# Half-array products for the query's low part in a hybrid attention layer

## The chip, the cores and the metric

The kernel runs on one NeuronCore of a Trainium2 chip. The metric is the device time of one execution in microseconds, the median of several executions. Five engines work side by side, each through a queue of its own: TensorE (PE, with its weight loads shown apart as PEld), VectorE (DVE), ScalarE (ACT), GpSimd (POOL) and SyncE (SP), which issues the transfers here.

## What is computed

One decoder layer over 2048 tokens of 1024 channels: a normalised and modulated `h`, one input projection of 4096 columns, two kinds of causal attention, an output projection and a gated residual. Eight heads of 64 use stick-breaking attention, four heads use differential attention, whose two maps have queries and keys of 64 each.

```python
def _stick_breaking(q, k, v):
        z = jnp.einsum('bhqd,bhkd->bhqk', qb, kf) * inv
        mask = spos[None, :] < tpos[:, None]
        log_1m = jnp.where(mask, jax.nn.log_sigmoid(-z), 0.0)
        rem = lax.cumsum(log_1m, axis=3, reverse=True) - log_1m
        a = jnp.where(mask, jnp.exp(jax.nn.log_sigmoid(z) + rem), 0.0)
        return jnp.einsum('bhqk,bhkd->bhqd', a, vf)

def _diff_attention(q1, q2, k1, k2, v, lam, slopes):
        s1 = jnp.einsum('bhqd,bhkd->bhqk', qb1, k1f) * inv + bias
        s2 = jnp.einsum('bhqd,bhkd->bhqk', qb2, k2f) * inv + bias
        p1 = jax.nn.softmax(jnp.where(mask, s1, -jnp.inf), axis=-1)
        p2 = jax.nn.softmax(jnp.where(mask, s2, -jnp.inf), axis=-1)
        return jnp.einsum('bhqk,bhkd->bhqd', p1 - lam * p2, vf)
```

## The kernel before

All large products take float32r operands. To keep precision each value is split into a high part (rounded to float32r) and a low part (the remainder), and products of parts are added in PSUM. `split_store` makes the two parts of projected queries and keys and writes them to DRAM (`qst`, `kst`); `ev_qk` calls it for the stick-breaking heads, `ev_dqk` for the differential ones. The tokens are worked on in two halves of 1024, and each half in chunks (`ch`) of 512.

`load_k` brings one chunk of 512 keys as a tile `kc` of 128 rows: 64 rows of the high part, below them 64 rows of the low part. `load_q` brings a pair of query tiles twice, on rows 0 to 63 and on rows 64 to 127, with the high part in slot 0 and the low part in slot 1. So in `scores` (L482) one product with slot 0 as weights gives q-high times (k-high + k-low) over all 128 rows, and a second one with slot 1 adds q-low times (k-high + k-low). In the stick-breaking heads the chunk on the diagonal gets a third product (L485), 128 wide, of an identity with a mask. Each product has its own weight load.

A row is one tile of 128 queries `i` against its `(i + 1) * 128` keys, in up to four chunks of up to 512 keys (`segs`; a last piece of 128 is computed 256 wide). The scores of a chunk lie in `ps_z`, a PSUM tile with three buffers (`NZ`). In the stick-breaking heads (`SBHead.front`) the chunks run from the last to the first; ScalarE makes two sigmoids of a chunk (L613, L614), VectorE scans it (L617), which is the last reader of `ps_z`, and GpSimd multiplies (L621). In the differential heads (`DFHead.front`) they run from the first to the last, and VectorE adds the bias and takes the maximum (L699), the only reader.

When two rows (a pair of query tiles) are done, `back_steps` turns the weights by 128x128 transposes into `ps_t` (L518), splits them into `aH` and `aL` (L524 on ScalarE, L525 on VectorE), and multiplies by the values into `av` (`vmm`: L598 and L599, or L671 to L673), 256 columns for two query tiles at a time. For the last key tile of a pair the first 128 columns belong to queries ahead of the keys; there `aH` and `aL` are set to zero by two memsets on GpSimd (L522, L523).

The order is set in two steps. A planner at the end of `build` lists the attention steps (`A`), each with a cost, and lets steps of the projections (`P`) in between by due times; `aper` sums an estimate of PE's time over the attention steps that issue a product, and projection steps are tied behind the product issued about `WINDOW` (17 us) earlier. Then the framework's scheduler orders each engine's queue by a forecast of its own. On the chip each queue runs in that order.

Of the kernel before, what the change touches and what calls it, by code (L numbers as in the profile page):

```python
# [7 lines left out]
F32 = mybir.dt.float32  # L8
# [37 lines left out]
def build(ctx: ExitStack, tc, xT, cT, normg, w_adaT, b_ada, w_in, qg, kg, lam4, subg, w_out,  # L46
          identd, distd, outT):
    nc = tc.nc
# [7 lines left out]
    zps = ctx.enter_context(tc.tile_pool(name="zps", bufs=NZ, space=PSUM))  # L56
# [12 lines left out]
    identr = ctile([128, 128], "ident", F32R)  # L69
# [12 lines left out]
    maskr = ctile([128, 128], "maskr", F32R)  # L82
# [270 lines left out]
    def ev_qk(dst, base):  # L353
        def f(ps, c, half, ch):
            p = (c - base) // 128
            t = dst[p][half]
            split_store(ps, [t[:, i, :, ch * 512:ch * 512 + 512] for i in range(2)])
        return f

    def ev_gate(ps, c, half, ch):  # L360
# [59 lines left out]
    def ev_dqk(isq):  # L420
        state = {}

        def f(ps, c, half, b2):
            qn = stage("qn")
            nc.scalar.copy(qn, ps)
            sq = stage("sq")
            nc.scalar.activation(sq, ps, AF.Square)
            if b2 % 2 == 0:
                state["ss"] = col.tile([128, 16], F32, name="qss", tag="qss", bufs=2)
                state["t"] = []  # L430
            ss = state["ss"]
            nc.vector.reduce_sum(out=ss[:, (b2 % 2) * 8:(b2 % 2) * 8 + 8],
                                 in_=sq.rearrange("p (u d) -> p u d", d=64), axis=AX.X)
            state["t"].append(qn)
            if b2 % 2 == 0:
                return
            v = col.tile([128, 16], F32, name="qv", tag="qv", bufs=1)
            nc.vector.tensor_scalar(out=v, in0=ss, scalar1=1.0 / 64, scalar2=EPS,
                                    op0=ALU.mult, op1=ALU.add)
            y = rsqrt(v, 16)  # L440
            tl = state["t"]
            for i in range(2):
                q3 = tl[i].rearrange("p (u d) -> p u d", d=64)
                nc.gpsimd.tensor_tensor(out=q3, in0=q3,
                                        in1=y[:, i * 8:i * 8 + 8].unsqueeze(2).broadcast_to([128, 8, 64]),
                                        op=ALU.mult)

            def finish(ch=b2 // 2):
                for s in range(2):
                    tp = pps.tile([128, 512], F32, name="ps_q", tag="pj")  # L450
                    for j in range(4):
                        o = (j % 2) * 256 + s * 128
                        nc.tensor.transpose(tp[:, j * 128:(j + 1) * 128], tl[j // 2][:, o:o + 128],
                                            ident)
                    hd = (c - (C_DFQ if isq else C_DFK)) // 128 + s
                    t = (qst if isq else kst)[4 + hd][half]
                    split_store(tp, [t[:, i, :, ch * 512:ch * 512 + 512] for i in range(2)],
                                qgain[:, hd:hd + 1] if isq else kgt[:, 0:1])
            pending.append([QK_DELAY, finish])
        return f  # L460
# [17 lines left out]
    def scores(q, kch, i, k0, w, diag=None):  # L478
# [7 lines left out]
                                          stop=True)  # L486
        return ps

    def segs(n, ext):
        return [(o, min(512, n - o), min(512, ext - o, max(256, n - o))) for o in range(0, n, 512)]  # L490

    def chunks(i):
        L = (i + 1) * 128
# [7 lines left out]
    def back_steps(pair, A, get_av, acol, vmm):  # L501
        i1 = 2 * pair + 1
        ng = i1 // 2 + 1

        def up(st, g):
            last = g == ng - 1
            tp = tps.tile([128, 512], F32, name="ps_t", tag="tr")
            aH = apool.tile([128, 512], F32R, name="aH", tag="aH", bufs=NA)
            aL = apool.tile([128, 512], F32R, name="aL", tag="aL", bufs=NA)
            blk = []  # L510
            for sl in range(2):
                sb = 2 * g + sl
                pos = (1 - sl) if last else sl
                blk.append((sb, pos * 256))
                for t in range(2):
                    if last and sl == 1 and t == 0:
                        continue
                    nc.tensor.transpose(tp[:, pos * 256 + t * 128:pos * 256 + t * 128 + 128],  # L518
                                        A[t][0][:, sb * 128:sb * 128 + 128], ident)
            f0 = 128 if last else 0  # L520
            if last:
                nc.gpsimd.memset(aH[:, 0:128].bitcast(F32), 0.0)  # L522
                nc.gpsimd.memset(aL[:, 0:128].bitcast(F32), 0.0)  # L523
            nc.scalar.copy(aH[:, f0:], tp[:, f0:])  # L524
            nc.vector.tensor_tensor(out=aL[:, f0:], in0=tp[:, f0:], in1=aH[:, f0:].bitcast(F32),  # L525
                                    op=ALU.subtract)
            st["h"] = (blk, aH, aL)

        def down(st, gi):
            av = get_av()  # L530
            blk, aH, aL = st["h"]
            for bi, (sb, o) in enumerate(blk):
                vmm(av[:, acol:acol + 256], sb, aH[:, o:o + 256], aL[:, o:o + 256],
                    gi == 0 and bi == 0, gi == ng - 1 and bi == 1)

        res = []
        sts = [{} for _ in range(ng)]
        for gi in range(ng + PIPE):
            def step(gi=gi):
                if gi < ng:  # L540
                    up(sts[gi], ng - 1 - gi)
                if gi >= PIPE:
                    down(sts[gi - PIPE], gi - PIPE)
            res.append((0.62 if gi < ng else 0.0, step))
        return res
# [34 lines left out]
    class SBHead(Head):  # L580
# [15 lines left out]
        def vmm(self, o, sb, aH, aL, st, sp):  # L596
            v = self.vch[sb // 4][:, sb % 4]
            nc.tensor.matmul(o, lhsT=v, rhs=aH, start=st, stop=False)  # L598
            last_pe[0] = nc.tensor.matmul(o, lhsT=v, rhs=aL, start=False, stop=sp)  # L599

        def front(self, i, A):
            steps = []
            tiles = {}

            def step(c0, w, we, first):
                self.open()
                q = self.get_q(i // 2)
                if first:
                    tiles["u"], tiles["s"] = self.row("u", i), self.row("s", i)
                u, s = tiles["u"], tiles["s"]  # L610
                dg = i * 128 - c0
                ps = scores(q, self.kch, i, c0, we, dg if 0 <= dg < w else None)
                nc.scalar.activation(s[:, c0:c0 + w], ps[:, :w], AF.Sigmoid, scale=0.125)  # L613
                nc.scalar.activation(ps[:, :w], ps[:, :w], AF.Sigmoid, scale=-0.125)  # L614
                top = c0 + w == L
                ur = ps[:, :w][:, ::-1]
                nc.vector.tensor_tensor_scan(out=u[:, c0:c0 + w][:, ::-1], data0=ur, data1=dist[:, :w],  # L617
                                             initial=1.0 if top else u[:, c0 + w:c0 + w + 1],
                                             op0=ALU.mult, op1=ALU.bypass)
                m = w - 1 if top else w  # L620
                nc.gpsimd.tensor_tensor(out=s[:, c0:c0 + m], in0=s[:, c0:c0 + m],  # L621
                                        in1=u[:, c0 + 1:c0 + m + 1], op=ALU.mult)

            L = (i + 1) * 128
            ext = (i // 2 + 1) * 256
            for si, (c0, w, we) in enumerate(reversed(segs(L, ext))):
                steps.append((2 * w / 960, lambda c0=c0, w=w, we=we, f=si == 0: step(c0, w, we, f)))

            def mid():
                A[0] = tiles["s"]  # L630
            return steps, (0.2, mid)
# [20 lines left out]
    class DFHead(Head):  # L652
# [27 lines left out]
        def front(self, i, A):  # L680
# [3 lines left out]
            nk = len(cl)  # L684
            ns = (128 * i + 639) // 512
            st = {}
            e = [None, None]

            def step(m, ci, c0, o, w, we, first):
                self.open()  # L690
                q = self.get_q(i // 2)[m]
                if "mx" not in st:
                    st["mx"] = col.tile([128, 2, ns], F32, name="mx", tag="mx")
                if first:
                    e[m] = self.row(f"e{m}", i)
                ps = scores(q, self.kch[m], i, c0 + o, we)
                d0 = 1920 - 128 * i + c0 + o
                j = (c0 + o) // 512
                nc.vector.tensor_tensor_reduce(  # L699
                    out=e[m][:, c0 + o:c0 + o + w], in0=ps[:, :w], in1=dist[:, d0:d0 + w], scale=1.0,  # L700
                    scalar=-3e38, op0=ALU.add, op1=ALU.max, accum_out=st["mx"][:, m, j:j + 1])
# [513 lines left out]
```

## Time and profile before

| | us |
|---|---|
| median of 3 executions | 1756.36 (1751.09 to 1757.32) |
| the profiled execution | 1752.65 |
| its span, first to last instruction | 1750.9 |
| busy: PE, PE's weight loads | 1657.7, 1486.7 |
| busy: VectorE, ScalarE, GpSimd | 1258.4, 990.3, 890.0 |

The stages in order of time: a start of 137 us, stick-breaking heads of half 0 up to 475 us, differential heads of half 0 up to 718, stick-breaking heads of half 1 up to 1250, differential heads of half 1 up to 1642, and a tail. Projections run beside the attention throughout. Recorded ends of matmuls are modelled; starts are what to read.

### The profile page before, as it was taken

How to read it: one execution, taken by the hardware profiler on the slowest of the kernel's cores; microseconds unless marked ns; L12 is line 12 of the kernel's file. 1: busy time of each engine (PE TensorE's matmuls, PEld its weight loads, DVE VectorE, ACT ScalarE, POOL GpSimd, SP SyncE). 2: the span in 40 equal slices, each digit the busy share in tenths (PEclk: the TensorE clock that was granted, in tenths of full speed). 3: DMA queues.
4: the chain of work that ended last, by engine and by line, in shares of the span. 5: the costliest groups of instructions: out<-in, count | busy, mean ns of one | idle time of the engine just before them, and what ended most of it. 6: DMA issues, size and time to landing. Idle time of an engine off the chain costs nothing.

```text
span 1750.9 us, 31674 instructions
## 1 busy us (share of the span) xinstructions
PE 1657.7 (95%) x10740; PEld 1486.7 (85%) x10740; DVE 1258.4 (72%) x2558; ACT 990.3 (57%) x1997; POOL 890.0 (51%) x1454
## 2 busy tenths in 40 slices
PE   1889989999999999999999999999999999999999
PEld 1677879789999989878898888799998988888887
DVE  6735645776657786767787877878888888888741
ACT  2335555555645444656776777777765645555521
POOL 5425464556635663565655655667433353323553
PEclk7999999999999999999999999999999999999999
DMA  7757767653564876434433333234433566434264
GB/s 254 228 151 211 217 187 226 190 163 85 164 181 135 254 240 187 157 106 121 121 101 105 97 109 97 79 94 131 133 88 116 162 204 203 130 127 134 86 216 149
DMA packets 212689, 268.65 MB, mean 153 GB/s; under 512 B 21296, under 2 KB 136240, under 8 KB 212400
## 3 DMA queue, kind: packets, MB, share of 16 engines
q1 hardware_dynamic: 212528, 266.64, 50.5%
q8 instruction: 85, 1.39, 0.3%
q14 instruction: 76, 0.62, 0.1%
HBM read 186.86 MB, written 79.69 MB: 152 GB/s over the span
## 4 chain that ended last, share of the span: by engine, by line
PE 69%; DVE 6%; DMA 4%; POOL 3%; issue 3%; ACT 2%; SPq 0%; DVEq 0%; ACTq 0%; POOLq 0%
PE ps_z L482 11%; PE ps_t L518 8%; PE ps_n L318 6%; PE ps_n L320 6%; PE ps_n L319 6%; PE ps_p L318 4%; PE ps_p L320 4%; PE ps_p L319 4%; PE av L599 3%; PE av L598 3%; PE ps_o L319 3%; PE ps_o L318 3%; PE ps_o L320 3%; PE av L672 1%; DMA xt<-in_xT 1%
## 5 line engine op out<-in xcount | busy, mean ns | idle before, releaser
L621 POOL TENSOR_TENSOR s<-s,u 128x512 f32<-128x512 f32 (+4 forms) x320 | 307.2, 962 | 213.1 <-DVE u L617 190.0
L482 PE MATMUL ps_z<-kc,qc 128*128 128x512 f32 (+2 forms) x1280 | 360.3, 376 | 9.4 <-DVE u L617 6.9
L524 ACT CAST aH<-ps_t 128x512 fp32r<-128x512 f32 (+1 forms) x432 | 240.7, 567 | 169.3 <-PE ps_t L518 159.5
L525 DVE TENSOR_TENSOR aL<-ps_t,aH 128x512 fp32r<-128x512 f32 (+1 forms) x432 | 276.3, 650 | 76.3 <-ACT aH L524 74.3
L318 PE MATMUL ps_n<-wh,hH 128*128 128x256 f32 x960 | 274.4, 286 | 2.4 <-DVE sl L327 1.2
L306 POOL TENSOR_TENSOR wl<-raw,wh 128x512 fp32r<-128x512 f32 x168 | 225.8, 1352 | 93.2 <-ACT wh L302 85.4
L319 PE MATMUL ps_n<-wl,hH 128*128 128x256 f32 x960 | 271.6, 284 | 1.0 <-POOL wl L306 1.0
L320 PE MATMUL ps_n<-wh,hL 128*128 128x256 f32 x960 | 272.3, 284 | 0.0
L617 DVE TENSOR_TENSOR_SCAN u<-ps_z,u,dist 128x512 f32<-128x512 f32 x192 | 245.6, 1279 | 33.8 <-ACT ps_z L614 27.7
L482 PEld LDWEIGHTS ps_z<-kc,qc 128*128 128x128 f32 x1280 | 210.9, 189 | 36.5 <-DVE u L617 11.9
L713 ACT ACTIVATE e<-e,nm 128x1024 f32<-128x1024 f32 (+4 forms) x192 | 171.9, 898 | 116.4 <-DVE nm L711 109.0
L699 DVE CUSTOM_DVE_ANT_0 e<-ps_z,dist 128x512 f32<-128x512 f32 (+3 forms) x320 | 186.9, 603 | 52.0 <-PE ps_z L482 44.5
L613 ACT ACTIVATE s<-ps_z 128x512 f32<-128x512 f32 (+3 forms) x320 | 172.9, 540 | 75.6 <-PE ps_z L482 38.9
L318 PE MATMUL ps_p<-hH,wh 128*128 128x512 f32 x480 | 192.5, 405 | 12.0 <-issue 11.2
L319 PE MATMUL ps_p<-hL,wh 128*128 128x512 f32 x480 | 189.7, 395 | 3.7 <-DVE hL L251 2.3
L320 PE MATMUL ps_p<-hH,wl 128*128 128x512 f32 x480 | 189.2, 395 | 0.0
L318 PEld LDWEIGHTS ps_n<-wh,hH 128*128 128x128 f32 x960 | 183.0, 191 | 6.9 <-issue 1.6
L319 PEld LDWEIGHTS ps_n<-wl,hH 128*128 128x128 f32 x960 | 183.2, 191 | 4.5 <-POOL wl L306 1.2
L320 PEld LDWEIGHTS ps_n<-wh,hL 128*128 128x128 f32 x960 | 183.3, 191 | 1.7
L614 ACT ACTIVATE ps_z<-ps_z 128x512 f32<-128x512 f32 (+3 forms) x320 | 173.2, 541 | 0.0
L518 PE MATMUL ps_t<-ident,s 128*128 128x128 f32 x1088 | 167.6, 274 | 5.2 <-DVE aL L525 4.9
L598 PE MATMUL av<-aH,vc 128*128 128x256 f32 x576 | 162.5, 294 | 7.4 <-ACT aH L524 6.3
(171 smaller groups left out, 3500.3 us busy)
## 6 DMA issues: line engine op xcount, KB each, us to landing
qc<-qst SPq DMA_DIRECT2D x256, 128.0 KB, 3.2
raw<-in_w_in SPq DMA_DIRECT2D x124, 256.0 KB, 3.3
kc<-kst SPq DMA_DIRECT2D x96, 256.0 KB, 3.5
xt<-in_xT SPq DMA_DIRECT2D x48, 256.0 KB, 4.7
vc<-vst SPq DMA_DIRECT2D x48, 256.0 KB, 3.1
vc<-vdt SPq DMA_DIRECT2D x48, 256.0 KB, 3.6
raw<-in_w_out SPq DMA_DIRECT2D x48, 256.0 KB, 3.4
wada<-in_w_adaT SPq DMA_DIRECT2D x16, 512.0 KB, 5.8
```

The source lines that it names most:

```text
L306: nc.gpsimd.tensor_tensor(out=wl, in0=raw, in1=wh.bitcast(F32), op=ALU.subtract)
L318: nc.tensor.matmul(ps, lhsT=aH, rhs=bH, start=first, stop=False)
L319: nc.tensor.matmul(ps, lhsT=aH, rhs=bL, start=False, stop=False)
L320: nc.tensor.matmul(ps, lhsT=aL, rhs=bH, start=False, stop=last)
L482: last_pe[0] = nc.tensor.matmul(ps[:, :w], lhsT=q[:, pt, tl], rhs=kch[k0 // 512][:, :w], start=pt == 0, stop=pt == 1 and diag is None)
L518: nc.tensor.transpose(tp[:, pos * 256 + t * 128:pos * 256 + t * 128 + 128], A[t][0][:, sb * 128:sb * 128 + 128], ident)
L524: nc.scalar.copy(aH[:, f0:], tp[:, f0:])
L525: nc.vector.tensor_tensor(out=aL[:, f0:], in0=tp[:, f0:], in1=aH[:, f0:].bitcast(F32), op=ALU.subtract)
L598: nc.tensor.matmul(o, lhsT=v, rhs=aH, start=st, stop=False)
L617: nc.vector.tensor_tensor_scan(out=u[:, c0:c0 + w][:, ::-1], data0=ur, data1=dist[:, :w], initial=1.0 if top else u[:, c0 + w:c0 + w + 1], ...
L621: nc.gpsimd.tensor_tensor(out=s[:, c0:c0 + m], in0=s[:, c0:c0 + m], in1=u[:, c0 + 1:c0 + m + 1], op=ALU.mult)
L699: nc.vector.tensor_tensor_reduce(out=e[m][:, c0 + o:c0 + o + w], in0=ps[:, :w], in1=dist[:, d0:d0 + w], scale=1.0, scalar=-3e38, op0=ALU.a ...
```

## The change

Odd chunks of keys are stored, and so loaded, with the low part on rows 0 to 63 and the high part on rows 64 to 127; even chunks stay as they were. A new function `scores2` takes an even and an odd neighbouring chunk together: two products with q-high over all 128 rows, then two with q-low, each over only the 64 rows that hold its chunk's high keys (rows 0 to 63 for the even one, 64 to 127 for the odd one). The product of both low parts is thereby left out for paired chunks. Both `ps_z` tiles are made at the first step of the pair; the second step finds its scores ready and issues no product. A chunk without a partner goes through `scores` as before. Row ends of 128 are computed 128 wide, and so is the product into `av` for a pair's last key tile, whose memsets go except where a pair has one group only.

```diff
--- before.py
+++ after.py
@@ ev_qk
-            split_store(ps, [t[:, i, :, ch * 512:ch * 512 + 512] for i in range(2)])
+            sw = ch if dst is kst else 0
+            split_store(ps, [t[:, i ^ sw, :, ch * 512:ch * 512 + 512] for i in range(2)])
@@ ev_dqk
-                    split_store(tp, [t[:, i, :, ch * 512:ch * 512 + 512] for i in range(2)],
+                    sw = 0 if isq else ch
+                    split_store(tp, [t[:, i ^ sw, :, ch * 512:ch * 512 + 512] for i in range(2)],
@@
+    def scores2(q, kch, i, parts, diag):
+        tl = slice((i % 2) * 128, (i % 2) * 128 + 128)
+        pss = {}
+        for k0, w in parts:
+            pss[k0] = zps.tile([128, 512], F32, name="ps_z", tag="z")
+            last_pe[0] = nc.tensor.matmul(pss[k0][:, :w], lhsT=q[:, 0, tl], rhs=kch[k0 // 512][:, :w],
+                                          start=True, stop=False)
+        for k0, w in parts:
+            r = slice(64 * (k0 // 512 % 2), 64 * (k0 // 512 % 2) + 64)
+            dg = diag - k0 if 0 <= diag - k0 < w else None
+            last_pe[0] = nc.tensor.matmul(pss[k0][:, :w], lhsT=q[r, 1, tl], rhs=kch[k0 // 512][r, :w],
+                                          start=False, stop=dg is None)
+        for k0, w in parts:
+            if 0 <= diag - k0 < w:
+                last_pe[0] = nc.tensor.matmul(pss[k0][:, diag - k0:diag - k0 + 128], lhsT=identr,
+                                              rhs=maskr, start=False, stop=True)
+        return pss
+
     def segs(n, ext):
-        return [(o, min(512, n - o), min(512, ext - o, max(256, n - o))) for o in range(0, n, 512)]
+        return [(o, min(512, n - o), min(512, n - o)) for o in range(0, n, 512)]
@@ back_steps
-            if last:
+            if last and ng == 1:
                 nc.gpsimd.memset(aH[:, 0:128].bitcast(F32), 0.0)
                 nc.gpsimd.memset(aL[:, 0:128].bitcast(F32), 0.0)
@@
-                vmm(av[:, acol:acol + 256], sb, aH[:, o:o + 256], aL[:, o:o + 256],
+                n0 = 128 if ng > 1 and gi == 0 and bi == 1 else 0
+                vmm(av[:, acol + n0:acol + 256], sb, aH[:, o + n0:o + 256], aL[:, o + n0:o + 256],
                     gi == 0 and bi == 0, gi == ng - 1 and bi == 1)
@@ SBHead.front
-                ps = scores(q, self.kch, i, c0, we, dg if 0 <= dg < w else None)
+                if c0 in ready:
+                    ps = ready.pop(c0)
+                elif c0 // 512 % 2:
+                    ready.update(scores2(q, self.kch, i, [(c0, w), (c0 - 512, 512)], i * 128))
+                    ps = ready.pop(c0)
+                else:
+                    ps = scores(q, self.kch, i, c0, we, dg if 0 <= dg < w else None)
@@ DFHead.front
-                ps = scores(q, self.kch[m], i, c0 + o, we)
+                k0 = c0 + o
+                if k0 in ready:
+                    ps = ready.pop(k0)
+                elif k0 // 512 % 2 == 0 and k0 + 512 < (i + 1) * 128:
+                    ready.update(scores2(q, self.kch[m], i, [(k0, w), (k0 + 512, min(512, (i + 1) * 128 - k0 - 512))],
+                                         -1))
+                    ps = ready.pop(k0)
+                else:
+                    ps = scores(q, self.kch[m], i, k0, we)
```

## Rows read from the trace of the kernel before

**Rows 1.** The page: busy time by engine (share), then 40 equal slices in tenths.
```profile
PE 1657.7 (95%) x10740; PEld 1486.7 (85%) x10740; DVE 1258.4 (72%) x2558; ACT 990.3 (57%) x1997; POOL 890.0 (51%) x1454
...
PE   1889989999999999999999999999999999999999
...
PEclk7999999999999999999999999999999999999999
```

**Rows 2.** Stages: start:end, length, busy us (xcount) by engine, granted clock, DMA.
```profile
core 0: us, PE busy (x) PEld busy (x) DVE busy (x) ACT busy (x) POOL busy (x), PEclk, DMA share, GB/s
...
137.00:475.00 338.00, 325.82 (x2090) 292.92 (x2089) 206.38 (x308) 190.81 (x403) 192.22 (x294) 0.99 0.61 178
475.00:718.00 243.00, 238.58 (x1710) 221.67 (x1709) 173.64 (x553) 124.54 (x268) 121.44 (x294) 1.00 0.67 197
718.00:1250.00 532.00, 519.58 (x3484) 468.26 (x3483) 419.81 (x521) 385.10 (x773) 325.76 (x437) 1.00 0.37 109
1250.00:1642.00 392.00, 384.38 (x2510) 345.22 (x2509) 340.96 (x965) 219.76 (x437) 141.32 (x305) 1.00 0.45 140
```

**Rows 3.** Waits of PE: who waited for whom, us in total, times, longest.
```profile
PE ps_z L482 <- DVE u L617: 6.9, 13, 0.7
...
PE ps_z L482 <- DVE mx L699: 2.2, 4, 0.9
```

**Rows 4.** PE's groups by shape: busy us, mean ns of one, idle before, releasers.
```profile
L482 PE MATMUL ps_z<-kc,qc 128*128 128x512 f32 x896 | 282.6, 404 | 8.4 <-DVE u L617 6.3 <-DVE mx L699 1.9
...
L482 PE MATMUL ps_z<-kc,qc 128*128 128x256 f32 x256 | 53.8, 291 | 1.1 <-DVE u L617 0.7 <-DVE mx L699 0.4
L482 PE MATMUL ps_z<-kc,qc 128*128 128x384 f32 x128 | 34.0, 344 | 0.0
```

**Rows 5.** Timeline of PE near 1001 us: start, us, instruction.
```profile
1000.12 0.39 PE L319 MATMUL ps_p<-hL,wh 128*128 128x512 f32 x1
1000.35 0.40 PE L320 MATMUL ps_p<-hH,wl 128*128 128x512 f32 x1
...
1001.96 0.39 PE L318 MATMUL ps_p<-hH,wh 128*128 128x512 f32 x1
```

**Rows 6.** Timeline of PE and its loads near 357 us.
```profile
356.89 0.23 PE L485 MATMUL ps_z<-maskr,ident 128*128 128x128 f32 x1
...
356.96 0.33 PE L598 MATMUL av<-aH,vc 128*128 128x256 f32 x1
357.01 0.19 PEld L599 LDWEIGHTS av<-aL,vc 128*128 128x128 f32 x1
357.13 0.28 PE L599 MATMUL av<-aL,vc 128*128 128x256 f32 x1
357.13 0.19 PEld L598 LDWEIGHTS av<-aH,vc 128*128 128x128 f32 x1
357.25 0.28 PE L598 MATMUL av<-aH,vc 128*128 128x256 f32 x1
357.25 0.19 PEld L599 LDWEIGHTS av<-aL,vc 128*128 128x128 f32 x1
357.36 0.28 PE L599 MATMUL av<-aL,vc 128*128 128x256 f32 x1
```

**Rows 7.** The first memset of `aH`: durations ns, idle before it, who waited.
```profile
L522 POOL MEMSET aH<- x96: 194/205/221, 0.7 to 1653.6; 128x128 f32 x96
...
  PE av L598: 64.0, 26
...
  ACT aH L524: 0.5, 1
```

**Rows 8.** Timeline near 773 us, stick-breaking, half 1: where two chunks of a row begin.
```profile
771.85 1.08 PE L482 MATMUL ps_z<-kc,qc 128*128 128x512 f32 x4
...
772.35 2.67 DVE L617 TENSOR_TENSOR_SCAN u<-ps_z,u,dist 128x512 f32<-128x512 f32 x2 [1.04 <-ACT ps_z L614]
...
773.68 0.73 PE L482 MATMUL ps_z<-kc,qc 128*128 128x512 f32 x2 [0.69 <-DVE u L617]
```

More of the change, by code (lines that the diff above doesn't have):

```diff
@@ L603, in front @@
             tiles = {}
+            ready = {}
             def step(c0, w, we, first):
@@ L686, in front @@
             st = {}
+            ready = {}
             e = [None, None]
```

## The prediction

> **What bounds the kernel now.** I read the page's busy shares first, then the same by stage, then who made TensorE wait, then single products in the timeline. TensorE (PE) is busy for 95% of the span, and from the second of the 40 slices on it stands at 8 or 9 tenths, with a granted clock of 9 tenths or more [rows 1]. By stage (stick-breaking heads of half 0, differential heads of half 0, then both for half 1) PE is busy 325.82 of 338, 238.58 of 243, 519.58 of 532 and 384.38 of 392 us, at a clock of 0.99 to 1.00, which is the 2.4 GHz level. VectorE is next, at most 340.96 of 392 us [rows 2]. All attention products lie in these 1505 us, so there a microsecond of PE is a microsecond of span, as long as no wait takes its place. Waits of PE at the score products are small today: 6.9 us for the scan and 2.2 us for the differential heads' reduction [rows 3].
>
> A record's duration is no price, since a 512-wide product is recorded at 404 ns and the next one starts long before that [rows 4]. The price is the distance between starts. Eight products of 512 columns from 1000.12 to 1001.96 us give 1.84/8 = 0.23 us each [rows 5]. Products of 256 columns stand at 357.13, 357.25 and 357.36: 0.12 us each, weight load included [rows 6]. For 384 I take the middle, 0.175. The 128-wide mask product is the interesting one. The product behind it starts 0.07 us later (356.89, 356.96), but that one's record is 0.33 instead of 0.28 us long and the next starts only at 357.13; the two together took 0.24, so the mask cost 0.12, as much as a product twice as wide [rows 6]. What held it is the load: each product has its own weight load, it starts as its predecessor's product starts (357.01, 357.13, 357.25), and a product cannot follow faster than one load, 0.12 us [rows 6].
>
> **The change part by part.** *Narrower products.* 64 row ends (128 wide instead of 256) and 196 products into `av` (84 pairs of query tiles; two products in a stick-breaking head, three in a differential one) lose 128 columns. By the columns alone they would give 0.06 us each, by the mask's row nothing, since the load sets the pace. The mask is the same kind of product, so I take nothing; the upper end is 324 narrower products (128 at row ends with both passes, 196 into `av`) x 0.06 = 19 us, the lower one 0. That no narrow product costs four times its columns is in the mask's row as well.
>
> *Memsets.* 84 of 96 pairs lose their two memsets on GpSimd. They last about 0.2 us each and one instruction of ScalarE waited for the first of them, 0.5 us [rows 7]. GpSimd is busy half of the time [rows 1], so this is worth 0 to 1 us; I take 0. GpSimd does idle 64.0 us ahead of the first one for older `av` products [rows 7]; that wait goes with the memset, and nobody on the path is shown to gain from it.
>
> *The low products.* There are 1280 score products (896 + 256 + 128), two for each of 640 chunks [rows 4]. Per stick-breaking head, and per map of a differential head, 16 rows of tiles hold 16 pairs of chunks: one in rows 4 to 7 and 8 to 11, two in rows 12 to 15. Over 16 heads and maps that is 256 pairs: in 160 both are 512 wide, and in 32 each the upper one is 384, 256 or 128. High products stay as they are. The two low products of a pair cost 0.46 us today (0.405 with 384, 0.35 with 256 or 128, which is padded to 256). Afterwards each uses 64 rows of the array. The trace of before has no product on part of the rows, so the price is bounded from both sides.
> - Wholly beside each other: the smaller one costs nothing. 160 x 0.23 + 32 x (0.175 + 0.12 + 0.12) = 50.1 us saved, half of it in each kind of head.
> - Second one started a load later: 0.12 + 0.23 = 0.35 instead of 0.46. In the differential heads (wide one first) this gives 0.11 for all 128 pairs, 14.1 us. In the stick-breaking heads the narrow one is first, so only 80 full pairs give 0.11, 16 give 0.055 and 32 nothing: 9.7 us. Together 23.8 us.
> - One after the other: 0.
> - And below: each change between whole and half array costs something (a rival, below).
>
> I take the second, because it is nearest to a row: every load in [rows 6] starts with the start of the product ahead of it, none two products ahead. The Trainium skill (TensorE: Matmul & The Clock Gate, section The mechanism) says more, that tiles in different row groups start about 4 ns apart and that a load for another row group is pulled ahead; by that sentence the sum is the 50.1 us of the first case. No run here shows it yet.
>
> *Two score buffers at once.* This is what the change adds. A pair needs two of the three `ps_z` buffers before its first low product can find its partner. I looked, for every pair, whether the reader two chunks back had ended when the pair's first product started: it had not in 11 of 32, 6 of 32, 50 of 96 and 28 of 96 pairs of the four stages, 95 of 256 in all, typically by 1 us. One of them stands in [rows 8]: four products from 771.85, the third of which (772.3) is the first of a pair and opens the third buffer, two scans up to 772.35 + 2.67 = 775.02, and the pair's second chunk only at 773.68, released by the first of these scans. In such pairs the second high product comes late; the scheduler, which orders PE's queue by its own forecast, then puts other work or the first low product ahead of it, and the two low ones no longer meet. So I let 67 of 128 stick-breaking and 94 of 128 differential pairs gain: 9.7 x 67/128 + 14.1 x 94/128 = 5.1 + 10.4 = 15.5 us. Behind a waiting second product, PE's whole queue stands: transposes of the last row, `av` products, projections. Today that costs the 9.1 us of [rows 3], and I add nothing in the forecast; the bound is in the rivals.
>
> *The rest.* A pair's first chunk is ready 0.35 us later than before (one high and a staggered low product more ahead of its reader), and its second one sooner. VectorE is idle for 51 to 131 us in every stage [rows 2], which covers the first; if that cover were gone, 128 stick-breaking pairs x 0.35 = 45 us would show, but then VectorE would be the bound, and it is not. Odd chunks change the place of two DMAs of equal size on SP; no transfer is added. The planner counts no PE time for the second step of a pair, so projection steps hang on slightly earlier attention products; PE hardly waits for that work now, and I give it 0, within 3 us either way.
>
> **Sum.** The profiled execution took 1752.65 us (span 1750.9), 3.7 below the median of 1756.36 of the runs shown. 1752.65 - 15.5 = 1737.2 on its own scale, 1740.9 on the median's. I say 1740.
>
> **The rivals.** *Full overlap.* The load of the second half passes the waiting first product. For it: the loads are hidden behind 512 columns everywhere, with 0.23 - 0.12 to spare [rows 5, 6]. Against it: no load in the rows starts before the product ahead of it. It gives 25.05 x (67 + 94)/128 = 31.5 us, about 1725; with all pairs adjacent 1706.
>
> *No overlap.* The products run one after the other, or nearly all pairs are pulled apart by the buffers. Sum 0 to 2 us: 1755. This is also how it looks if the change does not do what it says.
>
> *The buffers (slower).* One mechanism: PE in program order, the second high product waiting for the reader two chunks back, everything behind it standing. Cut at 2 us for the few that wait for longer, the 95 waits sum to 93 us. For it: [rows 8] show 0.69 us of PE idle for just this. Against it: this is only the largest kind, the whole kernel has 9.1 us of it [rows 3], since there is always other work to be put ahead. If half of the 93 us shows, 1756 - 15.5 + 46.5 = 1787. It decides from 15.5/95 = 0.16 us a pair.
>
> *Changing between whole and half array (slower).* If the array must be empty before its rows are split, two changes for a pair that stays together and four for one pulled apart make 161 x 2 + 95 x 4 = 702 changes. A record ends 0.39 - 0.23 = 0.16 us after the next could start [rows 5]; as an upper price that is 112 us. With a third of it, 0.05, it is 35 us: 1756 - 15.5 + 35 = 1776. It turns the sign from 15.5/702 = 22 ns on. No row shows a price, as nothing in the kernel before splits the array. The Trainium skill (TensorEngine Tiling (Array Packing), section Key Properties) speaks for this rival: "Changing tiling mode (not just tile) drains the TensorE"; it gives no time for that.
>
> **How the numbers follow.** Staggered overlap (1740; its own range 1730 to 1750) 0.34; full overlap (1706 to 1730) 0.24; no overlap (1750 to 1760) 0.16; buffers (1760 to 1800) 0.12; change of the array (1760 to 1850) 0.14. Half a per cent is 8.8 us, about what a measurement of this kernel can tell from no change: faster is below 1747.6, slower above 1765. The staggered case is faster but for a tenth of its chance: 0.34 - 0.04 + 0.24 + 0.03 (no overlap with gains from narrow products) = 0.57. Same: 0.04 + 0.12 + 0.02 + 0.02 = 0.20. Slower: the rest, 0.23. The range from 1710 to 1785 leaves out the best end of full overlap (0.06) and the dear ends of the last two rivals (0.12).
>
> **What would show it.** In the profile of the changed kernel the distance from the first low product to the second, where they stand side by side: 0.12 is the forecast, near 0 full overlap, 0.23 none. The distance from the last high product to the first low one, and from the last low one to the next whole product: over 0.23 + 0.02 is the price of splitting the array. The number of pairs that stand together: I count on 161 of 256. Waits of score products for the scan: 9 us today; over 25 us is the buffers' rival. The pace of a 128-wide `av` product: 0.12. The prediction is wrong if PE's busy time falls and another engine's work fills the span, or if the scheduler's new order makes PE wait in places that the sum does not touch.

## The result, and the profile after

The changed kernel takes 1895.29 us (1892.48 to 1899.1) against 1755.57 for the kernel before, 1.0798 times as long (95% interval 1.0777 to 1.0819). The forecast was 1740, and the range ended at 1785. The profiled executions stand at 1892.48 and 1752.65, 139.8 us apart.

The page of the changed kernel, to be laid beside [rows 1]: busy time by engine and the 40 slices.

```profile
PE 1817.0 (96%) x10740; PEld 1479.5 (78%) x10740; DVE 1275.9 (67%) x2558; ACT 993.4 (53%) x1995; POOL 858.8 (45%) x1286
...
PE   2899999999999999999999999999999999999999
...
PEclk7999999999999999999999999999999999999999
```

The number of products is the same, 10740, and so is the row of the granted clock, but PE is busy for 159 us more, and its weight loads cover 78% of the span where they covered 85%. The other engines are busy for much the same time as before. So the time was lost on PE itself, not in a wait for another engine. The waits of PE (who for whom, us in total, times, longest) say so as well; before they were those of [rows 3]:

```profile
PE ps_z L497 <- DVE u L647: 2.9, 3, 1.6
...
PE ps_z L484 <- DVE u L647: 1.3, 3, 0.6
PE ps_z L484 <- DVE mx L738: 1.0, 1, 1.0
```

5.2 us instead of 9.1. L497 are the high products of pairs, L502 the half-array low ones, L484 the chunks without a partner. Where the time went is seen in the starts. First a pair that stands together, two high products and two low ones (timeline of the changed kernel: start, us, instruction, idle before):

```profile
733.94 0.63 PE L497 MATMUL ps_z<-kc,qc 128*128 128x512 f32 x2
734.50 0.19 PEld L502 LDWEIGHTS ps_z<-kc,qc 64*128 64x128 f32 x2 [0.36 <-issue]
734.50 0.50 PE L502 MATMUL ps_z<-kc,qc 64*128 64x512 f32 x2
734.93 0.42 PEld L539 LDWEIGHTS ps_t<-ident,e 128*128 128x128 f32 x4 [0.25 <-issue]
734.93 0.55 PE L539 MATMUL ps_t<-ident,e 128*128 128x128 f32 x3
```

The two low products do run side by side: two records of 0.50 us merge into 0.50, and taken one by one their starts are 3 ns apart. Their two loads run side by side too, both within 0.19 us. But the load of the first one does not start with the product ahead of it, as the loads of [rows 6] do (within 0.05 us). It starts 0.56 us behind the start of the two high products (2 x 0.23 of them and 0.10 more), together with its own product, and the loads' row was idle for 0.36 us with nothing to wait for that the profile shows ("issue"). The same at the end: the next whole product, and its load, start 0.43 us behind the low ones, where 0.23 is the pace of [rows 5]. Now a low product alone, between whole ones:

```profile
752.33 0.44 PE L497 MATMUL ps_z<-kc,qc 128*128 128x512 f32 x1
752.70 0.18 PEld L502 LDWEIGHTS ps_z<-kc,qc 64*128 64x128 f32 x1 [0.24 <-issue]
752.70 0.50 PE L502 MATMUL ps_z<-kc,qc 64*128 64x512 f32 x1
753.13 0.19 PEld L319 LDWEIGHTS ps_p<-hL,wh 128*128 128x128 f32 x1 [0.25 <-issue]
753.13 0.50 PE L319 MATMUL ps_p<-hL,wh 128*128 128x512 f32 x1
753.23 0.19 PEld L320 LDWEIGHTS ps_p<-hH,wl 128*128 128x128 f32 x1
753.46 0.40 PE L320 MATMUL ps_p<-hH,wl 128*128 128x512 f32 x1
```

From the start of L502 to that of L319 0.43 us, and from L319 to L320 0.33 instead of 0.23, because L319's own load was not hidden. (The high product itself, at 752.33, is followed after 0.37; 0.06 of that is the narrow product ahead of it, as at the mask in [rows 6].) Between whole and half array, then, no product starts for about 0.10 us beyond what the columns need, and the load behind that takes another 0.10 us or so in the open, once on the way in and once on the way out.

Over the whole trace the 512 half-array products stand in 462 visits: 412 of one product and 50 of two. (A visit is a run of half-array products without a whole one between them.) All 206 pairs whose low products do not stand together have their score products in the same order, high, low, high, low. The run *The pairs without the half array*, below, has the same 10740 products in the same order with the low ones on the whole array, so I set the distance from each start to the next against it, product by product: 47 us more at the products ahead of a visit, 77 at the half products, 29 at the products behind a visit (where these are not also ahead of the next one), 153 in all or 0.33 a visit. What the 50 free partners give back is already in it. Everywhere else the distances are 24 us shorter, waits and gaps of PE that I did not take apart, and that leaves the 129 us between the two spans, 1890.7 and 1761.6.

### The profile page after: what moved, and what is told of

The parts are those of the page before. It is cut to its first block, busy times and chain, and to the rows that moved or that the text cites. A ratio compares the mean times of both kernels' runs of the same rounds, so it can differ in the third digit from the quotient of the medians.

```text
span 1890.7 us, 31419 instructions
## 1 busy us (share of the span) xinstructions
PE 1817.0 (96%) x10740; PEld 1479.5 (78%) x10740; DVE 1275.9 (67%) x2558; ACT 993.4 (53%) x1995; POOL 858.8 (45%) x1286
## 4 chain that ended last, share of the span: by engine, by line
PE 84%; DVE 6%; DMA 4%; ACT 2%; issue 2%; POOL 1%; SPq 1%; DVEq 0%; POOLq 0%; ACTq 0%
PE ps_z L502 9%; PE ps_t L539 9%; PE ps_n L318 7%; PE ps_n L320 6%; PE ps_n L319 6%; PE ps_z L497 6%; PE ps_p L318 6%; PE ps_p L320 5%; PE ps_p L319 5%; PE av L621 3%; PE av L622 3%; PE ps_o L318 3%; PE ps_o L319 3%; PE ps_o L320 3%; PE ps_z L484 2%; PE av L701 2%
## 5 line engine op out<-in xcount | busy, mean ns | idle before, releaser
L306 POOL TENSOR_TENSOR wl<-raw,wh 128x512 fp32r<-128x512 f32 x168 | 221.3, 1323 | 139.5 <-ACT wh L302 127.3
L318 PE MATMUL ps_n<-wh,hH 128*128 128x256 f32 x960 | 281.3, 294 | 0.0
L320 PE MATMUL ps_n<-wh,hL 128*128 128x256 f32 x960 | 275.0, 287 | 0.0
L319 PE MATMUL ps_n<-wl,hH 128*128 128x256 f32 x960 | 274.0, 286 | 0.0
L502 PE MATMUL ps_z<-kc,qc 64*128 64x512 f32 (+3 forms) x512 | 222.1, 475 | 0.0
L497 PE MATMUL ps_z<-kc,qc 128*128 128x512 f32 (+3 forms) x512 | 198.6, 402 | 3.5 <-DVE u L647 2.9
L319 PE MATMUL ps_p<-hL,wh 128*128 128x512 f32 x480 | 191.2, 399 | 3.7 <-DVE hL L251 2.2
L320 PE MATMUL ps_p<-hH,wl 128*128 128x512 f32 x480 | 191.4, 399 | 0.0
L320 PEld LDWEIGHTS ps_n<-wh,hL 128*128 128x128 f32 x960 | 183.6, 191 | 5.0 <-issue 4.8
L319 PEld LDWEIGHTS ps_n<-wl,hH 128*128 128x128 f32 x960 | 183.6, 192 | 5.0 <-issue 4.3
L502 PEld LDWEIGHTS ps_z<-kc,qc 64*128 64x128 f32 x512 | 84.8, 183 | 116.1 <-issue 111.5
```

The costliest lines, as they stand in the source:

```text
L306: nc.gpsimd.tensor_tensor(out=wl, in0=raw, in1=wh.bitcast(F32), op=ALU.subtract)
L318: nc.tensor.matmul(ps, lhsT=aH, rhs=bH, start=first, stop=False)
L319: nc.tensor.matmul(ps, lhsT=aH, rhs=bL, start=False, stop=False)
L320: nc.tensor.matmul(ps, lhsT=aL, rhs=bH, start=False, stop=last)
L497: last_pe[0] = nc.tensor.matmul(pss[k0][:, :w], lhsT=q[:, 0, tl], rhs=kch[k0 // 512][:, :w], start=True, stop=False)
L502: last_pe[0] = nc.tensor.matmul(pss[k0][:, :w], lhsT=q[r, 1, tl], rhs=kch[k0 // 512][r, :w], start=False, stop=dg is None)
```

## The experiments

Two theories. Theory 1: each visit to the half array has a fixed price, whatever stands around it. Theory 2: two score buffers at once and the new order of the queues cost the time.

**The price by itself.** A kernel that computes none of the layer, only products of one tile in fixed patterns. One of the patterns is shown; `whole` issues a product over 128 rows, `half` one over rows 0 to 63 (`lo`) or 64 to 127 (`hi`):

```diff
+    for _ in range(12):
+        whole("g_whole")
+        whole("g_whole")
+        half("g_half", lo)
+        half("g_half", hi)
```

> A kernel of its own that computes none of the layer: products of one 128x512 tile in fixed patterns, whole array (128 rows) and half array (64 rows), so that the distance between starts is the price. Theory 1 (splitting the array costs time at each visit to half-array products, 0.39 us by the trace of the changed kernel: 0.10 before the first half product, 0.19 behind the last and 0.10 at the whole product behind it): one whole and one half product take 2 x 0.23 + 0.39 = 0.85 us a round; two whole and two halves 2 x 0.23 + 0.23 + 0.39 = 1.08; four and four 4 x 0.23 + 2 x 0.23 + 0.39 = 1.77; eight and eight 3.14; halves alone, in turn on the lower and upper rows, 0.115 each. Theory 2 (the loss in the changed kernel comes from waits and from the order, not from the array): 0.46, 0.69, 1.38 and 2.76 for the four patterns. Whole products 256 and 128 wide one behind the other: 0.12 each if the weight load sets the pace, 0.06 for the narrow one if the columns do.

Its timeline (start, us for all, instruction, count), first the products without a change of the array:

```profile
16.47 5.60 PE L33 MATMUL a_whole<-k,q 128*128 128x512 f32 x24
21.91 3.04 PE L33 MATMUL b_whole<-k,q 128*128 128x256 f32 x24
24.78 2.80 PE L33 MATMUL c_whole<-k,q 128*128 128x128 f32 x24
27.41 2.94 PE L33 MATMUL d<-k,q 128*128 128x256 f32 x24
...
109.88 5.70 PE L36 MATMUL l_half<-k,q 64*128 64x512 f32 x46
115.50 5.73 PE L33 MATMUL m_whole<-k,q 128*128 128x512 f32 x24
```

By the starts, a whole product takes (21.91 - 16.47)/24 = 0.227 us with 512 columns, 0.120 with 256 and 0.110 with 128. Half products in turn on the lower and the upper rows take (115.50 - 109.88)/46 = 0.122 each, with the way back to the whole array in it; from the first of these starts to the last, taken one by one, it is 0.118 (0.115 was expected). Half products on the lower rows alone start 0.23 apart, like whole ones. The granted clock from 16.5 to 121 us is 1.00. Then one round of each pattern, and the loads of four half products:

```profile
30.98 0.50 PE L33 MATMUL e_whole<-k,q 128*128 128x512 f32 x1
31.41 0.50 PE L36 MATMUL e_half<-k,q 64*128 64x512 f32 x1
31.84 0.50 PE L33 MATMUL e_whole<-k,q 128*128 128x512 f32 x1
...
41.28 0.50 PE L33 MATMUL f_whole<-k,q 128*128 128x512 f32 x1
41.71 0.50 PE L36 MATMUL f_half<-k,q 64*128 64x512 f32 x2
42.15 0.50 PE L33 MATMUL f_whole<-k,q 128*128 128x512 f32 x1
...
51.90 0.73 PE L33 MATMUL g_whole<-k,q 128*128 128x512 f32 x2
52.56 0.49 PE L36 MATMUL g_half<-k,q 64*128 64x512 f32 x2
52.99 0.73 PE L33 MATMUL g_whole<-k,q 128*128 128x512 f32 x2
...
65.66 1.21 PE L33 MATMUL h_whole<-k,q 128*128 128x512 f32 x4
66.80 0.73 PE L36 MATMUL h_half<-k,q 64*128 64x512 f32 x4
67.47 1.21 PE L33 MATMUL h_whole<-k,q 128*128 128x512 f32 x4
...
88.74 2.11 PE L33 MATMUL i_whole<-k,q 128*128 128x512 f32 x8
90.78 1.20 PE L36 MATMUL i_half<-k,q 64*128 64x512 f32 x8
91.91 2.13 PE L33 MATMUL i_whole<-k,q 128*128 128x512 f32 x8
...
66.80 0.30 PEld L36 LDWEIGHTS h_half<-k,q 64*128 64x128 f32 x4 [0.37 <-PE h_whole L33]
```

One and one take 0.86 us a round (0.85 expected by theory 1, 0.46 by theory 2), two and two 1.09 (1.08, 0.69), four and four 1.81 (1.77, 1.38), eight and eight 3.17 (3.14, 2.76). One whole and two halves take 0.87, so the second half costs next to nothing. No other engine takes part here. A visit costs 1.09 - 3 x 0.227 = 0.41 us, and 3.17 - 12 x 0.227 = 0.45 with eight products, if each two of them are counted as one. That is theory 1, and it has a consequence: the pattern of the change, two high products and a pair of low ones, takes 1.09, and four whole products take 4 x 0.227 = 0.91. A pair that stands together loses 0.18 us. Four half products in a visit are even (1.81 against 8 x 0.227 = 1.82), and of these patterns only the one with eight wins (3.17 against 3.63). The four loads of pattern h take 0.30 us together: one load is 0.19, so two of them start 0.11 behind the other two, and the loads of the two halves of the array do not wait for each other.

**The narrow products alone**, on the kernel before: `segs` and the product into `av` as in the change, memsets as in the change, no pairs (the edit in part; the product into `av` starts at column `n0`).

```diff
-        return [(o, min(512, n - o), min(512, ext - o, max(256, n - o))) for o in range(0, n, 512)]
+        return [(o, min(512, n - o), min(512, n - o)) for o in range(0, n, 512)]
...
-            if last:
+            if last and ng == 1:
...
+                n0 = 128 if ng > 1 and gi == 0 and bi == 1 else 0
```

> The kernel before with the row ends and the products for a pair's last key tile 128 wide and without the memsets; no pairs of chunks, no half-array products. If the weight load sets the pace of narrow products: 0 to 2 us less than before. If their columns do: 324 x 0.06 = 19 us less, about 1737.

Measured 1757.36 against 1757.82 us, ratio 1.0004 (0.9988 to 1.0021). A narrower product gains nothing, as the first of the two expectations has it, and the memsets were worth nothing that can be measured. (Pattern c above says the same, 0.110 against 0.120; its loads start 0.11 apart, one right behind the other.)

**The pairs without the half array.** The changed kernel with one line changed; the instructions stand in the same order on all five engines.

```diff
-            r = slice(64 * (k0 // 512 % 2), 64 * (k0 // 512 % 2) + 64)
+            r = slice(0, 128)
```

> The changed kernel with the low products over all 128 rows; every queue keeps the order of the changed kernel. Theory 1 (visits to half-array products): the loss is gone, 1740 to 1757. Theory 2 (two score buffers at once, and the new order): it stays above 1840.

Measured 1761.48 us, ratio 1.0018 (1.0002 to 1.0034). Page and low products of this kernel:

```profile
PE 1663.8 (94%) x10740; PEld 1494.6 (85%) x10740; DVE 1265.1 (72%) x2558; ACT 982.5 (56%) x1995; POOL 855.9 (49%) x1286
...
L502 PE MATMUL ps_z<-kc,qc 128*128 128x512 f32 x416 | 161.6, 397 | 0.0
```

Loads cover 85% of the span again, as in [rows 1]. The kernel before stood at 1757.82 beside it, so with the order and the buffers of the change the loss is 3.7 us of 140 (the interval gives 0.4 to 6); the other 136 hang on that one line. The time lies 4 us above the range that I expected from theory 1 and some 80 below theory 2's bound. Theory 2 falls as the cause of the loss.

**Both low products tied together.** The changed kernel with both low products held behind the second high one (the edit in part):

```diff
+        hi = last_pe[0]
...
+            with tc.issue_after(hi.ins):
+                last_pe[0] = nc.tensor.matmul(pss[k0][:, :w], lhsT=q[r, 1, tl],
+                                              rhs=kch[k0 // 512][r, :w], start=False, stop=dg is None)
```

> The changed kernel with both low products of a pair tied behind its second high product, so that all 256 pairs stand together and there are 256 visits instead of 462. Theory 1: a visit costs 0.39 and saves the smaller low product (50 us over all pairs): 256 x 0.39 - 50 = 50 us over before, 1795 to 1810. Rival (the loss comes from pairs pulled apart, and a pair that stands together gains): 1730 or less. Rival (buffers): the second high product now holds the queue, and waits for the scan or the reduction of over 25 us appear.

Measured 1799.23 us, ratio 1.0238 (1.0216 to 1.0259); 253 pairs stand together, in 259 visits. Two of its pairs, and its two largest waits at score products:

```profile
733.67 0.63 PE L497 MATMUL ps_z<-kc,qc 128*128 128x512 f32 x2
734.23 0.50 PE L504 MATMUL ps_z<-kc,qc 64*128 64x512 f32 x2
734.66 0.66 PE L198 MATMUL ps_c<-ident,osq 128*128 128x128 f32 x4
...
756.07 0.49 PE L504 MATMUL ps_z<-kc,qc 64*128 64x512 f32 x2
756.50 0.50 PE L319 MATMUL ps_p<-hL,wh 128*128 128x512 f32 x1
```

```profile
PE ps_z L497 <- DVE u L649: 9.9, 18, 1.8
...
PE ps_z L497 <- DVE mx L740: 3.0, 4, 2.1
```

Nearly every pair now has its partner for nothing, and the kernel is still 41 us slower than before (1757.82 beside it), within 9 us of theory 1's 50 and in its range. The buffers' rival wanted over 25 us of waits; these are 13. Standing together is worth 98 of the 140 us (140 - 41), but no gain is left at the end of it.

**One visit for each low product**, without pairs (the edit in part; `half` is true for the chunks that had a partner, and `scores2` is not called):

```diff
+            if half and pt == 1:
+                r = slice(64 * (k0 // 512 % 2), 64 * (k0 // 512 % 2) + 64)
...
```

> The changed kernel without pairs: each chunk makes its whole high product and at once its half-array low product (in the chunks that had a partner; the others stay whole), so there are up to 512 visits to the half array, one product each, and one score buffer at a time as before. Price by the visit, from the changed kernel (462 visits, 50 pairs together, 140 us) and from both low products tied together (256 visits, about 44 us over before): about 0.32 us a visit net of waits that it covers, so 512 visits give 150 to 200 us over before, 1905 to 1955. If pairing and its buffers had a share in the loss, it would be under 1895.

Measured 1912.91 us against 1750.96, ratio 1.0914 (1.0852 to 1.0977): 162 us for 512 visits, 0.32 each; its trace has 512 visits of one product. It lies in the range, and not under the 1895 at which pairing and its buffers would have had a share. The changed kernel gives (140 + 10)/462 = 0.32, and with its pairs together (41 + 50)/259 = 0.35 (50 us is the first bound of the prediction's sum, what the partners save). So visits are what counts, at 0.32 to 0.35 each here; what is left to the 0.41 of the patterns I did not take apart, beyond the 24 us (0.05 a visit) by which the changed kernel's other distances shrank.

**Four score buffers**, to see why only 50 pairs stand together, and the same buffers without the change:

```diff
-NZ, NT, NP = 3, 2, 2
+NZ, NT, NP = 4, 1, 2
```

> The changed kernel with four score buffers (and one transpose buffer instead of two, since PSUM has eight banks). If the pairs are pulled apart for want of a second score buffer, far more than 50 of 256 now stand together, and the time falls by 0.4 us or more for each. If the scheduler puts the first low product ahead of the second high one for its own reasons, the number of pairs together does not rise, and the time over the same buffers without the change is again 130 to 160 us.

> The kernel before with four score buffers and one transpose buffer: the control for the changed kernel with these buffers. Within 3% of before, either way: a fourth score buffer takes waits for the scan away (9 us), one transpose buffer adds waits of TensorE for ScalarE and VectorE.

Measured 2190.61 and 2139.00 us. My expectation for the control, within 3% of before, was far off: the two buffer counts together cost 22%, and the largest waits point to the one transpose buffer:

```profile
PE av L598 <- ACT aH L524: 56.9, 77, 3.4
PE ps_t L518 <- DVE aL L525: 48.8, 103, 2.9
PE ps_z L482 <- DVE u L617: 41.5, 83, 2.1
```

The control's granted clock is lower as well, 0.94 on average against 0.99, and PE is busy for 86% of its span against 95%. The difference of 52 us misses the 130 to 160 that I expected, and with so much idle time on PE it is no price. As to the order, with a fourth buffer 31 pairs stand together, fewer than 50. That alone is weak, since the transposes' buffer changed with it; but with both low products tied, three buffers were enough for 253 pairs at 13 us of waits. So a pair does not need a fourth buffer to stand together. The scheduler puts the first low product ahead of the second high one when nothing forces it otherwise; why its forecast prefers that I did not find out.

## Why the prediction was wrong

- *What bounds the kernel* was right: PE was busy for 159 us more, and the execution took 140 longer. It only had the other sign.
- *Narrower products and memsets at nothing* was right, and the mask's row was the right one to read: 1.0004.
- *The price of the low products.* I took a start one load (0.12 us) behind the first, and it is 3 ns: full overlap, a rival at 0.24, was right on the overlap itself. Every load in [rows 6] was one for the whole array, and these do stand 0.12 apart; two loads for different halves of the array take 0.19 us together, so here they set no pace.
- *The failed step is the change between whole and half array*, which the sum had at nothing and the rivals at 0.05 us for each of 702 changes, with 0.16 as the upper price. It is about 0.20 a change in the patterns (0.41 a visit) and 0.17 in the kernel (153 us for 924 changes, two for each of 462 visits). My upper price came near that, but it rested on the tail of a record alone, whose end is modelled, and the rival's 1776 took a third of it; I left out that the load of the other kind cannot be hidden behind the product ahead of it. [Rows 6] showed that the hidden load is what gives 0.12 and 0.23, and I used that for the narrow products and not here. The Trainium skill's sentence that a change of tiling mode drains the engine (TensorEngine Tiling (Array Packing), Key Properties) agrees with the patterns, where each change adds 0.10 us before the next load can start; the price stands in the runs alone.
- *The chance of that rival*, 0.14, was too small. The gain of a pair was 0.11 us by my own sum, so it turned the sign from 22 ns a change on, and I had no row that put the price under that. A gain that small against an unknown price on each side of it wanted a chance nearer a half.
- *Pairs standing together.* I counted on 161 of 256 and there were 50. The reason that I gave, that the second high product must wait for a buffer, is not borne out: three buffers held 253 pairs together once they were tied, and a fourth one gave 31. What else pulls them apart stays open. This step cost 98 us of the 140 (41 are left with the pairs together), but it does not turn the sign.
- *The buffers* were no rival: 4 us with the pairs on the whole array, the new order in it, and 13 us of waits with the pairs tied together.

## What to carry to other kernels

A product on part of the rows is not priced by its columns but by its visit: here 0.41 us to leave the whole array and come back, so a visit has to save more than that, which with 512-wide products in two halves took more than four of them in one visit (four were even, eight won). Before splitting the array, count how often the queue goes in and out of it, in the order that the scheduler really builds, and look for what hides the weight load of the first product on either side. If a price that a change adds twice at each place is shown by no row, measure it with a few dozen products before anything else, since a gain of 0.1 us at each place is turned by 50 ns on each side.

## What the runs showed of the hardware

- Two products on rows 0 to 63 and rows 64 to 127, into different buffers, start 3 ns apart and cost the time of one (0.87 us a round with two beside a whole one, 0.86 with one), and their loads run side by side; a long stream of them runs at 0.118 us each, against 0.227 for a whole one of 512 columns. On the lower rows alone it is 0.23 each, and nothing is saved.
- Between a whole and a half-array product the next weight load starts only together with its own product: 0.43 us from start to start instead of 0.23, with 512 columns.
- A whole product of 128 columns takes 0.110 us, one of 256 columns 0.120: the loads of the 128-wide ones follow each other every 0.11 us, and half the columns save 0.01.
